# A two-layer encoder trunk: input in column pieces, later sums of the activations, attention's projection ahead of the convolution's

## The chip, the core and the metric

The kernel runs on one core of a Trainium2 chip. The metric is the device time of one execution in microseconds (us). Engines are called PE (TensorE), ACT (ScalarE), DVE (VectorE), POOL (GpSimd) and SP (SyncE, which issues most of the loads). Each takes its own instructions in order and waits for the others by semaphores.

## The reference

The input x has 512 rows of 1024 float32. Two layers, each with two feed-forward networks (FFN) around a mixer of attention and convolution:

```python
def reference(x, ...):
    for l in range(2):
        x = x + 0.5 * swiglu_ffn(rmsnorm(x, ffn1_norm[l]), ffn1_w_up[l], ffn1_w_down[l])
        x = x + mixer(rmsnorm(x, mix_norm[l]), w_in[l], ...)
        x = x + 0.5 * swiglu_ffn(rmsnorm(x, ffn2_norm[l]), ffn2_w_up[l], ffn2_w_down[l])
        x = rmsnorm(x, final_norm[l])

def swiglu_ffn(h, w_up, w_down):          # w_up 1024 x 5632, w_down 2816 x 1024
    a, b = split(h @ w_up); return (silu(a) * b) @ w_down

def mixer(h, ...):
    q, k, v, glu_in, gates = split(h @ w_in + b_in)
    outs, lses = dilated window attention of 3 groups of 8 heads (rms-normed, rotated q and k)
    wts = softmax over the 3 groups of lses
    y_attn = sum(wts * outs) (512 x 512) @ w_attn_proj (512 x 1024)
    y_conv = silu(layernorm(depthwise_conv31(glu))) @ w_conv_proj (1024 x 1024) + b_conv_proj
    g_attn, g_conv = split(sigmoid(gates))
    return (g_attn * y_attn + g_conv * y_conv) @ w_out
```

## The kernel before

**Layout.** The activations are held transposed, as eight tiles x0 to x7 of 128 features by 512 rows. Each activation that enters a product is split into a high and a low part (xgh and xgl, sh and sl for y, zh and zl for the convolution's result), made by ACT (a rounding copy, `hi`) and DVE (the difference, `lo`), and every weight tile too (`stage`: SP loads `raw`, ACT makes `hi`, DVE makes `lo`). A product is then three matmuls (`mm3`, L157 to L159). `proj_cols` runs such products for 256 columns of a weight at once, into two PSUM banks. The high and low parts of the weights have four buffers each, `raw` has two. A norm's scale is applied behind a product: R is the reciprocal root of the row's mean square, made by DVE and ACT and spread over the partitions by a matmul (`ps_bc`, L214).

**Start.** Four row tiles `xnat` (128 x 1024) are loaded by SP (L80), PE transposes them (`ps_x`, L721), ACT and DVE make xgh and xgl from the transposed banks (L174, L175), ACT squares the row tiles for the first norm (`sqn`, L727).

**FFN** (`ffn`). The up-projection is walked in pairs of column tiles m = 0, 2, 4 ... 20, in three PARTS of which each ends with its share of the down-projection. For m below 4 both halves a and b are plain products (banks `ps_a`, `ps_b`). From m = 4 on b is made by a seven-product scheme (`proj7`, banks `ps`), which needs sums of four quarter tiles of the activation: `sums7` (L269 to L271), from g = xgh + xgl (L324), split into Th and Tl; and likewise sums of the weights (`stage7`, `sm`, L251 to L253). After a pair DVE multiplies ps_a by R (L340), ACT applies silu, DVE multiplies by b (L345 or L343), and the result h is split. Layer 1's first FFN also runs `deferred`, the rescaling of x0 to x7 by the norm at the end of layer 0 (L780), behind the pair m = 0.

**Mixer** (`mixer`). Products with w_in and the attention of the three groups fill most of it; the convolution's 31 taps run on DVE meanwhile. Attention's unnormed results are written to device memory as `od`, twelve blocks of 128 x 512 (group by pair of heads), and come back at the end. That end, the combining of the heads, is: PE transposes the groups' weights (`ps_cT`, L665); ACT and DVE split them (`tmp`, L166 and L167); for each of four pairs of heads and three groups PE spreads the weights over the partitions (`ps_c`, two matmuls, L673 and L674), POOL loads a block of od into `oin` (L676, tag `ot` with four buffers), DVE multiplies (L677) and sums the three (L681); the sum is split into y (L166, L167). Then come the convolution's projection (`ps_cp`, 192 matmuls, needs z), whose product with the gate sgc stands at L689; attention's projection (`ps_ap`, 96 matmuls, needs y0 to y3), product with the gate sga (L698) and sum (L699), split into `mg`; and the output projection (`ps_o`).

**Order.** The code is written stage by stage; a scheduler places the instructions on the engines by priority (written order, with loads of weights and some norms pulled ahead), buffers of a pool and PSUM banks limit it. The placed order, not the written one, is what each engine runs.

## Time and profile before

| | us |
|---|---|
| median of three runs | 2653.77 (2652.79 to 2654.54) |
| the profiled execution | 2655.37 |
| its span in the trace | 2653.3 |
| PE busy in the span | 2593.0 |
| DVE busy | 1984.0 |
| ACT busy | 1100.8 |

The profile lists each instruction with its start, its duration, and, in brackets, how long its engine stood idle before it and which instruction or transfer ended that idle time. The ends of matmuls are modelled, so what one costs is read from the distance of two starts. PE waits have to be looked for one by one, since it is busy for 98% of the span.

### The profile page before, as it was taken

Reading aid. Unit: us, or ns where it says so; the run is one execution under the profiler, and the core shown is the slowest. Engines: PE = TensorE matmul, PEld = TensorE weight load, DVE = VectorE, ACT = ScalarE, POOL = GpSimd, SP = SyncE. Lnnn points to the kernel's source line nnn. Section 1 sums busy time; section 2 is a strip of 40 time slices with the busy share of each in tenths; the row PEclk is TensorE's granted clock in tenths of the full one; section 3 lists DMA queues with packets and bytes.
Section 4 is the critical chain, followed back from the end, with each engine's and each line's share of the span. In section 5 each row is a group of like instructions: output and inputs, shape, how many; then the busy total and the mean of one; then the engine's idle time right before and its main releaser. Section 6 shows DMA issues by size and latency. Waiting matters only on the chain.

```text
span 2653.3 us, 34486 instructions
## 1 busy us (share of the span) xinstructions
PE 2593.0 (98%) x13421; PEld 2168.9 (82%) x13421; DVE 1984.0 (75%) x3218; ACT 1100.8 (41%) x1651; POOL 110.8 (4%) x208
## 2 busy tenths in 40 slices
PE   8999999998999999999979999999999999999998
PEld 6888988776877788888868989887767777888887
DVE  6666669999986667666766766699999866666665
ACT  5333342243587234233433333422445773433334
POOL 1000000011011000000000000000011110000000
PEclk9999999999999999999989999999999999999999
DMA  4323333232333333232313333332323343233322
GB/s 143 104 92 108 92 108 105 84 119 89 108 108 113 111 96 104 88 111 91 101 55 111 96 104 96 103 105 88 110 88 120 104 129 104 88 104 96 108 92 80
DMA packets 245603, 268.87 MB, mean 101 GB/s; under 512 B 11624, under 2 KB 230128, under 8 KB 245440
## 3 DMA queue, kind: packets, MB, share of 16 engines
q1 hardware_dynamic: 233920, 234.91, 28.5%
q0 software_dynamic: 11504, 31.76, 4.1%
q8 instruction: 105, 1.72, 0.3%
q14 instruction: 58, 0.48, 0.1%
q10 hardware_dynamic: 16, 0.00, 0.0%
HBM read 251.75 MB, written 14.88 MB: 100 GB/s over the span
## 4 chain that ended last, share of the span: by engine, by line
PE 92%; DVE 6%; ACT 1%; issue 1%; DMA 0%; SPq 0%; ACTq 0%
PE ps_a L158 6%; PE ps_a L159 6%; PE ps_a L157 6%; PE ps_d L158 6%; PE ps_d L157 6%; PE ps_d L159 6%; PE ps L159 5%; PE ps L158 5%; PE ps L157 5%; PE ps_n L158 4%; PE ps_n L157 4%; PE ps_n L159 4%; DVE cv L620 2%; PE ps_S L528 1%; PE ps_pv L558 1%; PE ps_cp L158 1%
## 5 line engine op out<-in xcount | busy, mean ns | idle before, releaser
L152 ACT ACTIVATE hi<-raw 128x1024 fp32r<-128x1024 f32 (+1 forms) x376 | 391.5, 1042 | 698.1 <-PE ps_d L158 156.1
L153 DVE TENSOR_TENSOR lo<-raw,hi 128x1024 fp32r<-128x1024 f32 (+1 forms) x376 | 451.1, 1200 | 252.0 <-ACT hi L152 251.1
L620 DVE SCALAR_TENSOR_TENSOR cv<-u,cwc,cv 128x497 f32<-128x497 f32 (+14 forms) x480 | 335.8, 738 | 0.0
L157 PE MATMUL ps_a<-xgh,hi 128*128 128x512 f32 x704 | 275.7, 392 | 18.5 <-DVE t L340 16.2
L158 PE MATMUL ps_a<-xgl,hi 128*128 128x512 f32 x704 | 276.7, 393 | 0.6 <-DVE xgl L175 0.6
L159 PE MATMUL ps_a<-xgh,lo 128*128 128x512 f32 x704 | 276.2, 392 | 0.0
L158 PE MATMUL ps_d<-hl,hi 128*128 128x512 f32 x704 | 272.6, 389 | 0.0
L159 PE MATMUL ps_d<-hh,lo 128*128 128x512 f32 x704 | 272.6, 389 | 0.0
L157 PE MATMUL ps_d<-hh,hi 128*128 128x512 f32 x704 | 270.6, 389 | 0.0
L158 PE MATMUL ps_n<-lo,xgh 128*128 128x512 f32 x576 | 229.2, 398 | 4.2 <-DVE lo L153 4.2
L159 PE MATMUL ps_n<-hi,xgl 128*128 128x512 f32 x576 | 226.0, 393 | 0.0
L157 PE MATMUL ps_n<-hi,xgh 128*128 128x512 f32 x576 | 215.6, 396 | 4.6 <-DVE tmp L483 4.2
L157 PEld LDWEIGHTS ps_a<-xgh,hi 128*128 128x128 f32 x704 | 133.2, 189 | 46.2 <-DVE t L340 16.6
L158 PE MATMUL ps<-Tl,hi 128*128 128x256 f32 x576 | 163.0, 283 | 0.0
L159 PE MATMUL ps<-Th,lo 128*128 128x256 f32 x576 | 163.0, 283 | 0.0
L157 PE MATMUL ps<-Th,hi 128*128 128x256 f32 x576 | 162.8, 283 | 0.0
L159 PEld LDWEIGHTS ps_a<-xgh,lo 128*128 128x128 f32 x704 | 133.1, 189 | 28.4 <-issue 0.5
L158 PEld LDWEIGHTS ps_a<-xgl,hi 128*128 128x128 f32 x704 | 133.4, 190 | 27.6 <-DVE xgl L175 1.1
L157 PEld LDWEIGHTS ps_d<-hh,hi 128*128 128x128 f32 x704 | 132.2, 188 | 27.5
L159 PEld LDWEIGHTS ps_d<-hh,lo 128*128 128x128 f32 x704 | 132.1, 188 | 27.5
L158 PEld LDWEIGHTS ps_d<-hl,hi 128*128 128x128 f32 x704 | 132.1, 188 | 27.3
L166 ACT ACTIVATE hi<-sm 128x1024 fp32r<-128x1024 f32 x72 | 76.4, 1061 | 184.7 <-DVE sm L253 76.0
(266 smaller groups left out, 5506.5 us busy)
## 6 DMA issues: line engine op xcount, KB each, us to landing
raw<-in_ffn_w_up_dram SPq DMA_DIRECT2D x176, 512.0 KB, 3.5
raw<-in_w_in_dram SPq DMA_DIRECT2D x88, 512.0 KB, 3.7
raw<-in_ffn_w_down_dram SPq DMA_DIRECT2D x76, 512.0 KB, 3.4
raw<-in_w_in_dram SPq DMA_DIRECT2D x96, 256.0 KB, 3.2
raw<-in_w_conv_proj_dram SPq DMA_DIRECT2D x16, 512.0 KB, 3.4
raw<-in_w_out_dram SPq DMA_DIRECT2D x16, 512.0 KB, 3.4
vd<-tmp POOLq DMA_DIRECT2D x24, 256.0 KB, 2.4
od<-ot POOLq DMA_DIRECT2D x24, 256.0 KB, 3.2
```

The source lines that it names most:

```text
L152: nc.scalar.activation(hi[:, :m], raw[:, :m], AF.Copy)
L153: nc.vector.tensor_sub(lo[:, :m], raw[:, :m], hi[:, :m].bitcast(F32))
L157: nc.tensor.matmul(ps, ah, bh, start=first, stop=False)
L158: nc.tensor.matmul(ps, ah, bl, start=False, stop=False)
L159: nc.tensor.matmul(ps, al, bh, start=False, stop=last)
L166: nc.scalar.activation(hi, src, AF.Copy)
L528: nc.tensor.matmul(pS[e][:, w * n + lo:w * n + hi], qkT[hp, i, b * P:(b + 1) * P], qkT[hp, 2 + i, k0 + lo:k0 + hi], start=True, stop=True)
L558: nc.tensor.matmul(pv[e * 64:(e + 1) * 64, i, b - b2, :], V[b + j][:, (hh * UH + h) * HD:(hh * UH + h + 1) * HD], PT[e][:, (nj * w + j) * ...
L620: nc.vector.scalar_tensor_tensor(a[:, t0:t1], u[k][:, t0 + d:t1 + d], cw(l, j, k), a[:, t0:t1], op0=ALU.mult, op1=ALU.add)
```

## The change

Four edits. The input comes in four column pieces (all 512 rows, 256 columns each) of one tile instead of four row tiles. The sums of the activations for the seven-product scheme, in all four FFNs, are made behind the evacuation of the pair m = 0 instead of ahead of the first product, and the deferred rescale moves from behind m = 0 to behind m = 2. In the mixer, attention's projection is written ahead of the convolution's; its result is multiplied into the gate sga in place, and the convolution's evacuation then makes the merged sum. y0 to y3 and the low part of the merged result take other buffers (`sp`, `V`, `big`).

```diff
@@ -73,12 +73,12 @@
 
     x0s = ExitStack()
     x0 = x0s.enter_context(tc.tile_pool(name="x0", bufs=1))
-    xnat = []
-    for tt in range(TT):
-        t = x0.tile([P, D], F32, name=f"xnat{tt}")
-        with tc.high_priority():
-            nc.sync.dma_start(t, A["x"][0, tt * P:(tt + 1) * P, :])
-        xnat.append(t)
+    xn = x0.tile([P, TT, D], F32, name="xnat")
+    xsrc = A["x"][0].rearrange("(t p) d -> p t d", p=P)
+    with tc.high_priority():
+        for c in range(0, D, 256):
+            nc.sync.dma_start(xn[:, :, c:c + 256], xsrc[:, :, c:c + 256])
+    xnat = [xn[:, tt] for tt in range(TT)]
 
     grow = x0.tile([KD, P], F32, name="grow")
     nc.scalar.dma_start(grow, A["ffn1_norm"][0].rearrange("(k p) -> k p", p=P))
@@ -318,11 +318,6 @@
         with tc.tile_pool(name=uniq("ffn"), bufs=4) as fp:
             few.add(id(fp))
             x7 = []
-            for q in range(0, KD, 2):
-                t2 = fp.tile([P, 2, S], F32, tag="t2", name=uniq("g2"), bufs=2)
-                for j in range(2):
-                    nc.vector.tensor_add(t2[:, j], xg[q + j][0].bitcast(F32), xg[q + j][1].bitcast(F32))
-                x7.append(sums7(fp, t2, xg[q:q + 2], "T", 8))
             for m0, m1 in PARTS:
                 h = []
                 for m in range(m0, m1, 2):
@@ -346,7 +341,13 @@
                     h2 = split_to(*(fp.tile([P, 2, S], F32R, tag="h", name=uniq("h" + x), bufs=8) for x in "hl"), t2)
                     for j in range(2):
                         h.append(tuple(x[:, j] for x in h2))
-                    if m == 0 and deferred is not None:
+                    if m == 0:
+                        for q in range(0, KD, 2):
+                            t2 = fp.tile([P, 2, S], F32, tag="t2", name=uniq("g2"), bufs=2)
+                            for j in range(2):
+                                nc.vector.tensor_add(t2[:, j], xg[q + j][0].bitcast(F32), xg[q + j][1].bitcast(F32))
+                            x7.append(sums7(fp, t2, xg[q:q + 2], "T", 8))
+                    if m == 2 and deferred is not None:
                         deferred()
                 last = m1 == NF
 
@@ -679,29 +680,23 @@
                         acc = o
                     else:
                         nc.vector.tensor_add(acc, acc, o)
-                y.append(split(mp, acc, "big", NB))
-
+                y.append(split(mp, acc, *(("sp", 6) if pr < 3 else ("V", 5))))
+
+            for c in range(4):
+                ps = [ps_at(uniq("ps_ap")) for _ in range(2)]
+                proj_cols(wap, c * 256, y, 4, ps)
+                for j in range(2):
+                    nc.vector.tensor_mul(sga[2 * c + j], ps[j], sga[2 * c + j])
+            mg = []
             for c in range(4):
                 ps = [(ps_at if c % 2 else ps_mm)(uniq("ps_cp")) for _ in range(2)]
                 proj_cols(wcp, c * 256, z, KD, ps)
                 for j in range(2):
                     k = 2 * c + j
-                    nc.vector.scalar_tensor_tensor(sgc[k], ps[j], pc("b_conv_proj", l, k), sgc[k], op0=ALU.add, op1=ALU.mult)
-            mg = []
-            for c in range(4):
-                ps = [ps_at(uniq("ps_ap")) for _ in range(2)]
-                proj_cols(wap, c * 256, y, 4, ps)
-                ss = []
-                for j in range(2):
-                    k = 2 * c + j
                     s = slot("tmp", 7)
-                    nc.vector.tensor_mul(s, ps[j], sga[k])
-                    nc.vector.tensor_add(s, s, sgc[k])
-                    ss.append(s)
-                if c % 2 == 0:
-                    ml = mp.tile([P, 4, S], F32R, tag="qk", name=uniq("ml"), bufs=2)
-                for j in range(2):
-                    mg.append(split_to(slot("sgc", 8, F32R), ml[:, 2 * (c % 2) + j], ss[j]))
+                    nc.vector.scalar_tensor_tensor(s, ps[j], pc("b_conv_proj", l, k), sgc[k], op0=ALU.add, op1=ALU.mult)
+                    nc.vector.tensor_add(s, s, sga[k])
+                    mg.append(split_to(slot("sgc", 8, F32R), slot("big", NB, F32R, name="ml"), s))
             for ts in ((0, 1), (2, 3), (4, 5), (6,), (7,)):
                 ps = [(ps_at if ts[0] in (0, 4, 7) else ps_mm)(uniq("ps_o")) for _ in ts]
                 proj_cols(wou, ts[0] * P, mg, KD, ps)
```

PE's order in the mixer of layer 0, where the heads are combined. Before, from the last products of the gate (ps_gA) over the transposes (ps_cT) into the convolution's projection:

```order
L158 MATMUL ps_gA_6735<-xgl_3152,hi_6767 128x512
L159 MATMUL ps_gA_6735<-xgh_3151,lo_6768 128x512
L665 MATMUL ps_cT_7185<-ident,cg_7165 96x128 x4
L157 MATMUL ps_cp_7290<-zh_7117,hi_7293 128x512
L158 MATMUL ps_cp_7290<-zl_7118,hi_7293 128x512
L159 MATMUL ps_cp_7290<-zh_7117,lo_7294 128x512
L157 MATMUL ps_cp_7290<-zh_7123,hi_7293 128x512
L158 MATMUL ps_cp_7290<-zl_7124,hi_7293 128x512
```

After, the same place:

```order
L159 MATMUL ps_gA_6732<-xgh_3148,lo_6765 128x512
L666 MATMUL ps_cT_7182<-ident,cg_7162 96x128 x4
L674 MATMUL ps_c_7191<-tmp_7187,sel 128x512
L674 MATMUL ps_c_7197<-tmp_7187,sel 128x512
L674 MATMUL ps_c_7204<-tmp_7187,sel 128x512
L674 MATMUL ps_c_7215<-tmp_7187,sel 128x512
L675 MATMUL ps_c_7191<-tmp_7188,sel 128x512
L675 MATMUL ps_c_7197<-tmp_7188,sel 128x512
L675 MATMUL ps_c_7204<-tmp_7188,sel 128x512
L675 MATMUL ps_c_7215<-tmp_7188,sel 128x512
```

The convolution's matmuls that followed the transposes are gone from here: the spreading of the weights now comes directly behind, all 24 in a row. Before, the first ps_c came 28 matmuls later, and the others stood among ps_cp's.

PE's order a little further on, after; sh and sl are the parts of y0 (7211, 7212) and y1 (7235, 7236):

```order
L674 MATMUL ps_c_7276<-tmp_7187,sel 128x512
L675 MATMUL ps_c_7276<-tmp_7188,sel 128x512
L157 MATMUL ps_ap_7287<-sh_7211,hi_7290 128x512
L158 MATMUL ps_ap_7287<-sl_7212,hi_7290 128x512
L159 MATMUL ps_ap_7287<-sh_7211,lo_7291 128x512
L157 MATMUL ps_ap_7287<-sh_7235,hi_7290 128x512
L158 MATMUL ps_ap_7287<-sl_7236,hi_7290 128x512
```

Behind the last ps_c the attention projection begins; ps_cp, 192 matmuls, stands behind it except for one (in layer 1 four) of them.

DVE's order at the start of layer 1's first FFN, from the spread norm's diagonals (dg) on. Before:

```order
L212 TENSOR_SCALAR dg_11015<-ident,rsr_10990 128x128 x4
L153 TENSOR_TENSOR lo_11309<-raw_11307,hi_11308 128x1024
L324 TENSOR_TENSOR g_1821_11026<-xgh_10734,xgl_10735 128x512
L324 TENSOR_TENSOR g_1821_11026<-xgh_10745,xgl_10746 128x512
L324 TENSOR_TENSOR g_1825_11037<-xgh_10808,xgl_10809 128x512
L324 TENSOR_TENSOR g_1825_11037<-xgh_10821,xgl_10822 128x512
L251 TENSOR_TENSOR sm_11353<-raw_11352 128x512
L780 SCALAR_TENSOR_TENSOR x_81<-x_81,pcol,ps_bc_11020 128x512
```

After:

```order
L212 TENSOR_SCALAR dg_11018<-ident,rsr_10993 128x128 x4
L153 TENSOR_TENSOR lo_11304<-raw_11302,hi_11303 128x1024
L251 TENSOR_TENSOR sm_11356<-raw_11355 128x512
L335 TENSOR_TENSOR t_1843_11153<-ps_a_11029,R_11016 128x512
L335 TENSOR_TENSOR t_1843_11153<-ps_a_11030,R_11016 128x512
L348 TENSOR_TENSOR g_1846_11164<-xgh_10737,xgl_10738 128x512
L348 TENSOR_TENSOR g_1846_11164<-xgh_10748,xgl_10749 128x512
L251 TENSOR_TENSOR sm_11412<-raw_11411 128x512
```

Two of the sums g of four stand now behind the evacuation of ps_a (L335, before L340), which before had its place 38 rows behind the first g (L324); the rescales (L780, now L775) follow in both.

ACT's order at the start of the kernel. Before:

```order
L152 ACTIVATE hi_304<-raw_303 128x1024
L727 ACTIVATE sqn_221,ss_220<-xnat_92 128x1024
L727 ACTIVATE sqn_223,ss_220<-xnat_94 128x1024
L727 ACTIVATE sqn_225,ss_220<-xnat_96 128x1024
L727 ACTIVATE sqn_227,ss_220<-xnat_98 128x1024
L152 ACTIVATE hi_334<-raw_333 128x1024
L174 ACTIVATE xgh_145<-ps_x_140,gcol 128x512
```

After:

```order
L152 ACTIVATE hi_257<-raw_256 128x1024
L152 ACTIVATE hi_287<-raw_286 128x1024
L174 ACTIVATE xgh_142<-ps_x_137,gcol 128x512
L174 ACTIVATE xgh_152<-ps_x_147,gcol 128x512
L718 ACTIVATE x_81<-ps_x_137 128x512
L174 ACTIVATE xgh_162<-ps_x_157,gcol 128x512
L718 ACTIVATE x_82<-ps_x_147 128x512
L174 ACTIVATE xgh_172<-ps_x_167,gcol 128x512
L722 ACTIVATE sqn_218,ss_217<-xnat 128x1024
```

The four squares of the row tiles stood ahead of the first xgh; now four xgh stand ahead of the first square, and a second weight tile is split ahead of them.

## Rows read from the trace of the kernel before

**Rows 1.** The page: busy us (share) xinstructions, then the last chain by engine.

```profile
PE 2593.0 (98%) x13421; PEld 2168.9 (82%) x13421; DVE 1984.0 (75%) x3218; ACT 1100.8 (41%) x1651; POOL 110.8 (4%) x208
...
PE 92%; DVE 6%; ACT 1%; issue 1%; DMA 0%; SPq 0%; ACTq 0%
```

**Rows 2.** Table by window: length, busy us (count) of PE, PEld, DVE, ACT, POOL; clock.

```profile
848.00:866.00 18.00, 18.00 (x80) 12.55 (x79) 13.43 (x19) 7.44 (x11) 1.62 (x3) 1.00 0.43 132
866.00:869.00 3.00, 3.00 (x9) 2.35 (x8) 1.60 (x4) 0.63 (x1) 1.08 (x2) 0.50 0.87 250
...
1368.00:1384.00 16.00, 4.91 (x12) 3.84 (x13) 15.85 (x28) 7.94 (x10) 0.00 (x0) 0.50 0.11 33
1384.00:1386.00 2.00, 2.00 (x9) 1.61 (x8) 1.48 (x2) 1.98 (x2) 0.00 (x0) 0.82 0.00 0
```

**Rows 3.** Timeline of ACT, then PE, at the start: start, duration, instruction.

```profile
4.48 1.06 ACT L152 ACTIVATE hi<-raw 128x1024 fp32r<-128x1024 f32 x1 [1.80 <-DMA raw<-in_ffn_w_up_dram]
...
9.27 1.06 ACT L727 ACTIVATE sqn<-xnat 128x1024 f32<-128x1024 f32 x1 [3.73 <-DMA xnat<-in_x_dram]
...
14.39 1.82 ACT L174 ACTIVATE xgh<-ps_x,gcol 128x512 fp32r<-128x512 f32 x3
...
9.29 3.54 PE L721 MATMUL ps_x<-ident,xnat 128*128 128x128 f32 x16 [5.64 <-DMA xnat<-in_x_dram]
15.12 0.73 PE L157 MATMUL ps_a<-xgh,hi 128*128 128x512 f32 x2 [2.28 <-ACT xgh L174]
```

**Rows 4.** DMA issues of the first 22 us: KB each, median us to landing.

```profile
raw<-in_ffn_w_up_dram SPq DMA_DIRECT2D x5, 512.0 KB, 5.6
xnat<-in_x_dram SPq DMA_DIRECT2D x4, 512.0 KB, 6.6
```

**Rows 5.** Timeline of PE, then DVE, at layer 1's first FFN.

```profile
1362.48 0.39 PE L159 MATMUL ps_b<-xgh,lo 128*128 128x512 f32 x1
1379.09 0.79 PE L157 MATMUL ps_a<-xgh,hi 128*128 128x512 f32 x1 [16.22 <-DVE t L340]
1379.68 0.63 PE L158 MATMUL ps_a<-xgl,hi 128*128 128x512 f32 x1
1380.11 0.63 PE L159 MATMUL ps_a<-xgh,lo 128*128 128x512 f32 x1
...
1356.09 2.50 DVE L324 TENSOR_TENSOR g<-xgh,xgl 128x512 f32<-128x512 f32 x4 [9.19 <-PE ps_bc L214]
...
1378.36 1.88 DVE L340 TENSOR_TENSOR t<-ps_a,R 128x512 f32<-128x512 f32 x3
...
1391.83 1.22 DVE L167 TENSOR_TENSOR hl<-t,hh 128x1024 fp32r<-128x1024 f32 x1
```

**Rows 6.** Timeline of PE, then DVE, combining the heads in layer 0.

```profile
848.38 0.60 PE L665 MATMUL ps_cT<-ident,cg 128*96 128x128 f32 x4
...
870.21 0.39 PE L159 MATMUL ps_cp<-zh,lo 128*128 128x512 f32 x1
870.43 0.39 PE L157 MATMUL ps_cp<-zh,hi 128*128 128x512 f32 x1
...
853.31 0.68 DVE L167 TENSOR_TENSOR tmp<-ps_cT,tmp 96x512 fp32r<-96x512 f32 x1
...
857.82 2.48 DVE L677 TENSOR_TENSOR oin<-oin,ps_c 128x512 f32<-128x512 f32 x4 [1.19 <-PE ps_c L674]
...
864.00 0.68 DVE L167 TENSOR_TENSOR sl<-oin,sh 128x512 fp32r<-128x512 f32 x1
...
884.40 0.69 DVE L167 TENSOR_TENSOR sl<-oin,sh 128x512 fp32r<-128x512 f32 x1 [0.70 <-ACT sh L166]
```

**Rows 7.** Loads of od: POOL's issue, DVE's product, landing times of all 24.

```profile
864.98 0.54 POOL L676 DMA_DIRECT2D oin<-od  x1 [1.86 <-DVE sl L167]
...
868.92 0.69 DVE L677 TENSOR_TENSOR oin<-oin,ps_c 128x512 f32<-128x512 f32 x1 [1.36 <-DMA oin<-od]
...
DMA to landing us min/median/max: 2.8/3.1/5.4
```

## The prediction

> **What bounds the kernel now.** I read the page's busy times first: TensorE (PE) works 2593.0 of 2653.3 us, VectorE (DVE) 1984.0, ScalarE (ACT) 1100.8, and the chain of work that ended last is 92% PE [rows 1]. So PE is the bound, and the change adds and removes no matmul: 13,421 stay. It can gain only where PE idles or runs at the lower clock, some 60 us in all, and can lose wherever it makes PE wait. Then I went stage by stage with the table of windows. PE is fully busy through the combining of the heads (18.00 of 18.00 us) [rows 2], so the mixer's edit has nothing to win there. Two holes touch the change: the start, and the beginning of layer 1's first FFN, where PE stood still for 16.22 us for a DVE evacuation [rows 5] and the clock was at half (granted 0.50) [rows 2].
>
> The steady price of one 128x512 matmul is the distance of two starts: 870.43 - 870.21 = 0.22 us (0.227 over a longer stretch) at full clock [rows 6], and 1380.11 - 1379.68 = 0.43 us at half [rows 5]. After that hole PE ran from 1379.09 and the granted clock was a mean 0.82 over 1384 to 1386: the rise came some 5.2 us after the restart [rows 2, 5].
>
> **The change, part 1: the input in column pieces.** Before, all of ps_x waits until 9.29 us for the row tiles of x, ACT then squares all four of them (first at 9.27), and only at 14.39 makes the first xgh, so the first projection matmul starts at 15.12 [rows 3]. With column pieces the first two transposable columns land before the rest, and in the new order ACT makes xgh ahead of the squares. A second weight load now goes ahead of x on SyncE's queue. The first weight tile's split began at 4.48 when it had landed, the four row tiles were there by 9.29 [rows 3], so a place of 512 KB in this queue costs about 1.2 us; I put the first piece at some 7 us, the second at 8.2, sixteen transposes end near 10 (0.22 us each, 3.54/16 [rows 3]), and the first matmul of ps_a comes 5 us sooner. The remaining transposes now stand between the matmuls, and ACT has the same 4 us of squares to do a little later, with PE's 24 first matmuls (some 8 us, partly at half clock) to cover them. I take 5 us gained; the ends are 0 (the pieces land together, the squares then hold xgh of the later columns back) and 8.
>
> A weight tile moves as 1 KB runs and x before as 4 KB runs, and both are 512 KB: 5.6 against 6.6 us from issue to landing [rows 4]. The short runs show no price here. The Trainium skill, "DMA: Bandwidth & Descriptors", section "Why small descriptors are slow (HBM only)", says against the change that each packet carries a fixed overhead of about three cycles beside one per 32 bytes. By it (an estimate) 35 cycles per KB against 131 per 4 KB make x 7% slower, some 0.3 us of the gain; the rows decide, and I take none.
>
> **Part 2: the sums of later activations behind the first evacuation.** Thirty-two adds and sixteen groups of differences in four FFNs change place; none is removed. At three of the starts PE had no idle time, so there is nothing to gain. At layer 1's first FFN the DVE begins its queue at 1356.09, when the broadcast of R arrives, and is then busy without a real break until hl at 1391.83 + 1.22 = 1393; in that queue the first evacuation of ps_a stands at 1378.36, behind 22 us of sums and rescales [rows 5]. The new order puts the two evacuations at some 1356.7, so PE goes on at 1362.7 instead of 1379.09. But the same some 35 us of DVE work must still be done, from the same start, and PE's next matmuls need its results: summed by the order with the durations of the trace (0.60 per 128x512 step, 1.14 per 128x1024), the last Tl is ready at about 1391, the bank evacuations of the next pair at 1383. After PE's 24 free matmuls and 4 more (6 us, until 1368.5) it advances in pieces. By about 1391 it can have done some 85 of the next 132 matmuls, and the rest (21 of 0.12 us, 26 of 0.227, with some waits for banks) end at 1400 to 1406, against 1408.4 before. I take 4 us gained, ends 0 and 9. The deferred rescale (eight steps, 5.3 us) stands in the same queue in both.
>
> **Part 3: the attention projection in front.** Before, behind the transposes of the head weights (848.38 to 848.98) PE has the convolution's projection to run while the chain of the heads goes its slow way: split of the weights (DVE until 853.99), the spread matmuls ps_c, products (857.82), sums, split of y0 (until 864.68), and so on to y3 at 884.40 + 0.69 = 885.09 [rows 6]. These 36 us cost PE nothing. In the new order the 24 ps_c follow the transposes at once, then the attention projection, which needs y0 to y3; the convolution's 192 matmuls, the cover, stand behind it. An engine takes its instructions in order, so PE waits.
>
> How long: ps_c can start at 854.0. Products of the first pair follow at about 854.9 (0.6 us each), sums end at 858.7, y0 is split by 860. Each further y needs loads of od into buffers that the y before releases: after sl ended at 864.68, GpSimd issued at 864.98 and the product followed at 868.92 [rows 6, 7], so 0.3 + 3.9 us, and with the median landing of 3.1 us [rows 7] some 3.4. A product and a sum more (1.3 us) make a step of 4.7 to 5.5 us; I take 5.3. Three steps from 858.7, and 1.3 us for the split: y3 at about 876. In before, y0 to y3 took 20.4 us with other work on DVE; that is the upper bound, y3 at 880.4. Thirty-one of the projection's 96 matmuls stand ahead of the first that needs y3, but their banks come free with the ninth product or later, so between 65 and 80 are left at 876. Either 12 of 65 at half clock (5.2 us) and 53 at 0.227, or 78 at 0.227: the projection ends at about 893.5. Without a wait the same work would end at 848.98 + 24 x 0.17 + 96 x 0.227 = 874.8. PE loses 18.7 us, less the 1.4 us that before already lost at half clock (866 to 869, granted 0.50 [rows 2], seven matmuls at 0.2 more): **17 us per layer**. Every microsecond of y3 is one of the loss: 14 with y3 at 873, 22 with 880.4. Layer 1 has the same chain with the same durations (the 24 loads of both layers stand in one row [rows 7]), so 34 us, from 28 to 44.
>
> The Trainium skill, "SBUF — State Buffer", section "The DMA setup-cost knee", gives a transfer some 2 us and its bytes by 436 GB/s: 2.6 us for these 256 KB (an estimate). By it a step would be 4.2 us, y3 at 873, and the sum 6 us lower. The rows show 2.8 at least and 3.1 in the median [rows 7]; they decide.
>
> The rest of the part is free: the convolution's projection, once begun, has z from before; its weights wait for staging buffers that the attention projection frees one by one, 5.4 us apart, ACT and DVE need 2.3 us per tile, and both have time there. The product into the gate in place removes no instruction. Attention's own stretch shifts by a few instructions: 0, ends -3 and 3.
>
> **Sum.** +34 - 4 - 5 = +25 us on 2655.37; the median of the runs is 1.6 us lower, so 2653.77 + 25 = 2679. Ends by the bounds: +28 - 9 - 8 - 3 = +8 and +44 + 3 = +47.
>
> **Rivals.** (a) *The hole in layer 1's FFN closes entirely*: PE never waits again once the bank is free, and gets back 16.22 us and the 12 half-clock matmuls (2.5 us): +34 - 19 - 5 = +10, 2664. For it: the hole's releaser is just the evacuation that moves. Against: the DVE's queue behind it. It decides if the last Tl is ready by 1372 rather than 1391.
> (b) *The faster side: y is ready before PE gets to it*, because the chain's loads run ahead of the sums that release their buffers and no hole opens: -4 - 5 = -9, 2645. It turns faster once the loss per layer is under 4.5 us, y3 by 863.5, that is three steps in 4 us. One load lands in 2.8 us at the least [rows 7] and the third step's waits for the second's sums, which speaks against it; only four buffers are there.
> (c) *The change does not do what it says*: the scheduler keeps convolution matmuls between the ps_c and the loss vanishes while the start gains nothing either: +0, 2654. The order of the new kernel shows no such matmul, so this has little left.
> (d) *The bubble costs more*, since the convolution's weights come late behind it or the attention stretch meets a new wait: 5 us per layer more, +35, 2689; inside the range.
>
> **How the numbers follow.** Forecast with (d) 0.76, (a) 0.10, (b) 0.08, (c) 0.06. About 0.2% (5.3 us) is what a measurement here can tell from no change. Faster: (b) and a little of (a) with the low ends, 0.10. Same: (c) and low ends, 0.07. Slower: 0.83. The range holds the forecast's bounds and (a) and leaves out (b), (c) and the last of the upper end: 2661 to 2697.
>
> **What would show it.** In the profile of the changed kernel: PE idle between about 849 and 876 us in layer 0 and again in layer 1 (shifted), released by DVE sl or the product, with a granted clock near 0.5 there, and some 60 matmuls of ps_ap after it; in layer 1's first FFN no 16 us wait on the evacuation but several smaller waits on Tl, lo and banks to about 1390; the first ps_a matmul near 10 us. The forecast is wrong if PE is over 90% busy in those two mixer stretches, or if y3 comes by 865.

## The result, and the profile after

The changed kernel takes 2686.07 us (median of four runs, 2684.43 to 2687.16) against 2654.02 us for the kernel before (median of four, the three of the table above and one more): **slower**, ratio 1.0121 (95% interval 1.0108 to 1.0133). The forecast of 2679 us with a range of 2661 to 2697 and 0.83 for slower holds. Its parts hold less well than its sum: one is 8 us too large, another 12 us too small.

The profiled execution took 2685.75 us (span 2683.4). Its busy times, which answer to [rows 1]:

```profile
PE 2606.8 (97%) x13421; PEld 2177.9 (81%) x13421; DVE 1987.1 (74%) x3218; ACT 1108.1 (41%) x1656; POOL 110.8 (4%) x208
```

PE has the same 13,421 matmuls, 13.8 us more busy time (the granted clock is at half for 95.7 us of the span, against 56.8) and, since the span grew by 30.1 us, 16.3 us more idle time. The table follows the same matmul in both traces: the first start of a stage's bank, after minus before, and what the stage in front of it added.

| first matmul of | before | after | difference | added by the stage |
|---|---|---|---|---|
| layer 0's mixer (ps_gg) | 373.2 | 370.1 | -3.1 | -3.1 start and first FFN |
| transposes of the head weights, layer 0 (ps_cT) | 848.4 | 849.1 | +0.8 | +3.9 attention, layer 0 |
| output projection, layer 0 (ps_o) | 923.6 | 936.7 | +13.2 | **+12.4** combining and projections |
| down-projection of layer 1's first FFN (ps_d) | 1429.3 | 1439.0 | +9.7 | -3.4 that FFN's beginning |
| ps_cT, layer 1 | 2167.9 | 2185.6 | +17.7 | **+8.0** attention, layer 1 |
| ps_o, layer 1 | 2241.5 | 2272.4 | +31.0 | **+13.2** combining and projections |
| end of the span | 2653.3 | 2683.4 | +30.1 | -0.8 |

The list of what PE waited for (engine line waited for: us in total, times, longest) names the same places. Before, its first row was the 16.22 us of [rows 5]; that row is gone:

```profile
PE ps_T L551 <- ACT sp L548: 11.7, 9, 2.9
PE ps_c L674 <- DVE oin L678: 9.0, 6, 3.5
...
PE ps_c L674 <- ACT tmp L166: 6.5, 2, 3.3
```

The waits of ps_c are the combining of the heads; ps_T, transposes in attention, had 5.9 us before.

**Combining the heads, layer 0.** PE's timeline (start, duration, instruction, idle before it and what ended it), which answers to [rows 6]:

```profile
849.14 0.60 PE L666 MATMUL ps_cT<-ident,cg 128*96 128x128 f32 x4
853.00 0.73 PE L674 MATMUL ps_c<-tmp,sel 8*128 8x512 f32 x4 [3.26 <-ACT tmp L166]
...
868.82 0.77 PE L157 MATMUL ps_ap<-sh,hi 128*128 128x512 f32 x1 [0.37 <-DVE oin L678]
...
893.22 0.39 PE L159 MATMUL ps_ap<-sh,lo 128*128 128x512 f32 x1
```

and the DVE's, with the products and the four splits of y:

```profile
855.63 2.48 DVE L678 TENSOR_TENSOR oin<-oin,ps_c 128x512 f32<-128x512 f32 x4 [0.89 <-PE ps_c L675]
...
860.13 0.69 DVE L167 TENSOR_TENSOR sl<-oin,sh 128x512 fp32r<-128x512 f32 x1 [0.69 <-ACT sh L166]
861.84 0.69 DVE L678 TENSOR_TENSOR oin<-oin,ps_c 128x512 f32<-128x512 f32 x1 [1.01 <-DMA oin<-od]
...
865.27 0.69 DVE L167 TENSOR_TENSOR sl<-oin,sh 128x512 fp32r<-128x512 f32 x1
...
870.09 0.69 DVE L167 TENSOR_TENSOR sl<-oin,sh 128x512 fp32r<-128x512 f32 x1
...
874.86 0.69 DVE L167 TENSOR_TENSOR sl<-oin,sh 128x512 fp32r<-128x512 f32 x1 [0.70 <-ACT sh L166]
```

PE transposes at 849.14, waits 3.26 us for the weights' split, then for products; y3 is split at 874.86 + 0.69 = 875.55, and the last matmul of the attention projection starts at 893.22. Before, PE ran the convolution's projection all that time. The table by window (length, busy us and count of PE, PEld, DVE, ACT, POOL, then the granted clock, the DMA share and GB/s) shows the price in clock:

```profile
849.00:854.00 5.00, 1.47 (x10) 0.68 (x8) 3.48 (x5) 4.55 (x8) 0.00 (x0) 0.98 0.03 11
854.00:869.00 15.00, 9.28 (x21) 4.70 (x22) 11.53 (x19) 1.26 (x2) 3.76 (x7) 0.50 0.46 140
869.00:874.00 5.00, 5.00 (x12) 3.96 (x13) 4.33 (x7) 0.63 (x1) 0.54 (x1) 0.50 0.38 105
874.00:878.00 4.00, 4.00 (x18) 3.28 (x17) 0.85 (x2) 0.63 (x1) 0.00 (x0) 0.97 0.00 0
```

In the 15 us from 854 PE is busy for 9.28, at half clock, and the clock stays there until 874, some 5 us after PE got steady work at 868.82.

**Layer 1's first FFN.** PE, and then the DVE, answering to [rows 5]:

```profile
1384.53 0.38 PE L157 MATMUL ps<-xgh,hi 128*128 128x256 f32 x1 [1.62 <-ACT hi L166]
...
1389.03 0.58 PE L159 MATMUL ps<-xgh,lo 128*128 128x256 f32 x1 [2.03 <-DVE lo L167]
...
1394.60 0.80 PE L157 MATMUL ps<-Th,hi 128*128 128x256 f32 x2 [1.47 <-ACT Th L166]
1397.38 0.58 PE L158 MATMUL ps<-Tl,hi 128*128 128x256 f32 x1 [1.99 <-DVE Tl L167]
```

```profile
1369.26 0.69 DVE L251 TENSOR_TENSOR sm<-raw 128x512 f32<-128x512 f32 x1 [9.20 <-PE ps_bc L214]
1369.87 1.28 DVE L335 TENSOR_TENSOR t<-ps_a,R 128x512 f32<-128x512 f32 x2
...
1403.19 1.22 DVE L167 TENSOR_TENSOR Tl<-ts,Th 128x1024 fp32r<-128x1024 f32 x1
```

One wait of 16.2 us has become seven of 0.5 to 2 us; the four longest rows are shown. The evacuation of ps_a now comes at 1369.87 right behind the broadcast, but the DVE's queue still runs from 1369.26 to the last Tl at 1403.19 + 1.22 = 1404.4, and PE waits for the queue's results one by one.

### The profile page after: what moved, and what is told of

It is laid out like the page before. It is cut to its first block, busy times and chain, and to the rows that moved or that the text cites. A ratio compares the mean times of both kernels' runs of the same rounds, so it can differ in the third digit from the quotient of the medians.

```text
span 2683.4 us, 34476 instructions
## 1 busy us (share of the span) xinstructions
PE 2606.8 (97%) x13421; PEld 2177.9 (81%) x13421; DVE 1987.1 (74%) x3218; ACT 1108.1 (41%) x1656; POOL 110.8 (4%) x208
## 4 chain that ended last, share of the span: by engine, by line
PE 60%; DVE 6%; ACT 1%; issue 1%; DMA 0%; DVEq 0%; SPq 0%; ACTq 0%
PE ps_d L158 4%; PE ps_d L159 4%; PE ps_d L157 4%; PE ps_a L158 4%; PE ps_a L157 4%; PE ps_a L159 4%; PE ps L158 3%; PE ps L159 3%; PE ps L157 3%; DVE cv L621 2%; PE ps_n L158 1%; PE ps_n L157 1%; PE ps_n L159 1%; PE ps_o L159 1%; PE ps_cp L159 1%; PE ps_cp L158 1%
## 5 line engine op out<-in xcount | busy, mean ns | idle before, releaser
L166 ACT ACTIVATE hi<-raw 128x1024 fp32r<-128x1024 f32 x72 | 76.4, 1060 | 197.7 <-PE ps_d L158 69.4
```

The costliest lines, as they stand in the source:

```text
L166: nc.scalar.activation(hi, src, AF.Copy)
```

## The experiments

The stage differences below are read as in the table, against the first trace of before.

### The mixer's edit undone, and alone

Undone (the code of before from y to the merged sum, the rest as changed):

```diff
-                y.append(split(mp, acc, *(("sp", 6) if pr < 3 else ("V", 5))))
+                y.append(split(mp, acc, "big", NB))
...
+            (convolution's projection, then attention's, as before)
```

> The changed kernel with the mixer's edit undone (input pieces, later sums and later rescale stay). In the trace of the changed kernel the start gained 3.1 us, layer 1's first FFN 3.5, the tail 0.9; the two stretches from the head weights' transposes to the output projection lost 12.4 and 13.2; attention's stretch lost 3.8 (layer 0) and 8.0 (layer 1). Theory A (the loss in attention comes from where the scheduler puts attention's matmuls, which shifts with any edit): layer 0 has PE's order of the changed kernel there and keeps the 3.8, layer 1 has an order of its own, 0 to 8 lost: 2654 - 7.5 + 3.8 to 11.8 = 2650 to 2658. Rival B (the loss in attention comes from the mixer's edit, by its buffers): both vanish, 2646.5. In both the two stretches behind the transposes show no idle PE.

Measured: 2652.8 us, ratio 0.9994 (0.9985 to 1.0004). Stages: start -2.6, attention of layer 0 +2.3, combining and projections -1.6 and 0.0, layer 1's FFN -4.8, attention of layer 1 +0.7.

Alone (the code of before, with the changed lines from y to the merged sum):

> The kernel before with the mixer's edit alone. Theory A: the 25.6 us behind the transposes, attention of layer 0 in the order of before (0), layer 1 in an order of its own (0 to 8): 2680 to 2688. Rival B: 25.6 + 11.8 = 2691.

Measured: 2685.48 us, ratio 1.0123 (1.0108 to 1.0138). Stages: combining and projections +12.2 and +13.6, attention +0.1 and +7.6. So the whole loss comes with the mixer's edit, and 25.7 us of it are in the stretch behind the transposes. The other edits take 9.5 us off the start, layer 1's FFN, the projections and the tail of this trace and add 3.0 in attention; but the profiled execution was the fastest of its ten (2648.92), and by the medians the kernel differs from before by no more than the measurement can tell. Both times lie where theory A put them. With the mixer's edit alone layer 0's attention did not lengthen, which speaks against rival B; layer 1 needed a run of its own.

### The convolution in front, the new buffers kept

```diff
             for c in range(4):
-                ps = [ps_at(uniq("ps_ap")) for _ in range(2)]
-                proj_cols(wap, c * 256, y, 4, ps)
+                ps = [(ps_at if c % 2 else ps_mm)(uniq("ps_cp")) for _ in range(2)]
+                proj_cols(wcp, c * 256, z, KD, ps)
...
-                proj_cols(wcp, c * 256, z, KD, ps)
+                proj_cols(wap, c * 256, y, 4, ps)
```

> The changed kernel with the convolution's projection in front again, while y, the low part of the merged result and the merged sum keep the new buffers. If the place of the projection is the cause of the stretch behind the transposes (theory), the time is that of the kernel without the mixer's edit within 2 us. If the new buffers cost time (rival: y in buffers shared with attention, the low part in those of the convolution's inputs), it lies above it by up to the 25 us.

Measured: 2651.93 us, ratio 0.9996 (0.9986 to 1.0005), 0.9 us from the kernel without the mixer's edit. Combining and projections: -1.6 and 0.0. The buffers are free; the place of the projection costs.

### Part of the cover put back, and the loads of od ahead

The first quarter of the convolution's projection in front of attention's, three quarters behind:

```diff
+            for c in range(1):
+                (projection and product with sgc of column pair c, in place)
             for c in range(4):
                 ps = [ps_at(uniq("ps_ap")) for _ in range(2)]
...
-            for c in range(4):
+            for c in range(1, 4):
```

> The changed kernel with the first quarter of the convolution's projection (48 matmuls, 10.9 us at full clock) ahead of attention's, the other three quarters behind it. Theory (PE has nothing to run while y0 to y3 are made): the quarter fills 10.9 us of the hole and keeps the clock up for some of it, so of the 12.4 and 13.2 us lost behind the transposes 1 to 4 are left in each layer: 2662 to 2670, layer 1's attention in another order again (-8 to +3 on that). Rival (the new place of the projection costs by its banks or weight buffers, not by a missing cover): the two stretches keep 10 us or more.

Measured: 2670.3 us, ratio 1.0064 (1.0047 to 1.008). The stretches lost 5.5 and 7.3 instead of 12.4 and 13.2: 48 matmuls of cover buy 7 and 6 us of their 10.9. More than the 1 to 4 us expected is left, since the chain itself became longer: the first products came at 857.28 instead of 855.63, behind matmuls of the quarter, and between them and y0 the DVE evacuated two banks of it (859.67 and 861.66, 0.74 us each) and split a weight tile (862.32, 1.22). y3 was ready at 878.70 + 0.69, 4 us later than in the changed kernel, and PE still waited for products:

```profile
PE ps_c L674 <- DVE oin L678: 5.6, 3, 2.7
```

The rival (10 us or more stay) falls. Then the chain itself, shortened. More buffers of `ot` have no room: with six, the mixer's pool needs 109.5 KB per partition where 106.6 are left. So the fifth to twelfth block go into the eight buffers that the convolution's results leave:

```diff
-                    o = slot("ot", 4, name="oin")
+                    o = slot("ot", 4, name="oin") if 3 * pr + g < 4 else slot("big", NB, name="oin")
```

> The changed kernel, but the fifth to twelfth block of attention's results go into the eight buffers that the convolution's results leave, so that all twelve loads stand ahead of the products. In the changed kernel y0 to y3 of layer 0 ended at 860.8, 866.0, 870.8 and 875.5. Theory of the prediction (each y waits for loads into buffers that the y before releases): what is left is DVE's own work, 12 products, 8 sums and 4 splits of 0.6 us from 855.6, some 14.4 us, so y3 at about 871 and 4 to 5 us less per layer: 2686 - 9 = 2677, apart from the order of attention's matmuls in layer 1, which is another one again (-8 to +3). Rival (loads are hidden, the chain is DVE's, ACT's and the spreading matmuls'): y3 stays within 1 us, 2686 apart from that order.

Measured: 2663.54 us, ratio 1.0039 (1.0024 to 1.0054). POOL's timeline: the loads now follow the splits of z, from 845.18, and the last one is issued before any product:

```profile
845.18 0.54 POOL L677 DMA_DIRECT2D oin<-od  x1 [1.58 <-DVE zl L167]
...
854.03 0.54 POOL L677 DMA_DIRECT2D oin<-od  x1 [1.20 <-DMA oin<-od]
```

and the DVE's splits of y0 to y3:

```profile
863.01 0.69 DVE L167 TENSOR_TENSOR sl<-oin,sh 128x512 fp32r<-128x512 f32 x1
...
866.01 0.69 DVE L167 TENSOR_TENSOR sl<-oin,sh 128x512 fp32r<-128x512 f32 x1
...
868.54 1.47 DVE L167 TENSOR_TENSOR sl<-oin,sh 128x512 fp32r<-128x512 f32 x2
```

The last row holds two, y2 and y3, so y3 is ready at 868.54 + 1.47 = 870.0 instead of 875.55, and the stretches lost 6.2 and 6.6 instead of 12.4 and 13.2. The loads that waited for buffers of the y before were thus half of the hole. The other half is the DVE's own 24 steps, which now follow each other with hardly a pause (busy 14.09 of the 15 us from 854); PE still waits 3.9 us for the weights' split and 0.9 us for products, and its clock is granted at a mean of 0.59 in these 15 us. The time fell by more than the 13 us of the two stretches because layer 1's attention came out in yet another order (0.0 instead of +8.0).

### Whose are the 8 us in attention?

The kernel before with the input's edit alone was run since its placed order of PE in layer 1's attention (the sequence of banks from the first ps_qT to ps_cT) is that of the changed kernel, with no edit of the mixer at all:

> The kernel before with the input in column pieces alone, no edit of FFN or mixer. Its placed order of attention in layer 1 is that of the changed kernel. Theory A (attention's loss of 8.0 us in layer 1 belongs to that order, whichever edit brings it about): the stretch from the first w_in product to the head weights' transposes is 6 to 9 us longer there than in before; the start gains 3; layer 0's attention has an order of its own, 0 to 4 longer: 2653 - 3 + 6 to 13 = 2656 to 2663. Rival B (it belongs to the mixer's buffers): layer 1's attention within 3 us of before and the time 2650 to 2654.

Measured: 2657.87 us, ratio 1.0013 (1.0004 to 1.0023). Layer 1's attention: +8.0 us, the same as in the changed kernel; start -4.8; layer 0's attention -1.8. What PE waited for in that stretch, before, changed, and here:

```profile
PE ps_T L550 <- ACT sp L547: 2.6, 3, 1.7
```

```profile
PE ps_T L551 <- ACT sp L548: 7.5, 5, 2.9
```

```profile
PE ps_T L550 <- ACT sp L547: 7.6, 6, 2.9
```

Theory A holds. PE waits for ACT's `sp` 5 us longer, and the other 3 us are busy time (371.15 us busy before, 374.36 changed, 374.71 here). That part stays open: the clock was at half for 13.7 us of this stretch both before and in the changed kernel. What the order does is seen at the longest of the waits, at the same transposes of the probabilities (those behind a row of 14 ps_pv), before and changed:

```profile
1966.33 3.38 DVE L620 SCALAR_TENSOR_TENSOR cv<-u,cwc,cv 128x510 f32<-128x510 f32 x5
...
1970.74 0.93 PE L550 MATMUL ps_T<-ident,sp 128*128 128x128 f32 x4 [0.28 <-ACT sp L547]
```

```profile
1976.17 6.00 DVE L621 SCALAR_TENSOR_TENSOR cv<-u,cwc,cv 128x508 f32<-128x508 f32 x9
...
1982.55 0.51 ACT L548 ACTIVATE sp<-sp,st 128x256 f32<-128x256 f32 x1 [3.38 <-DVE st L542]
...
1983.20 1.18 PE L551 MATMUL ps_T<-ident,sp 128*128 128x128 f32 x4 [2.90 <-ACT sp L548]
```

Nine of the convolution's taps (`cv`) instead of five stand on the DVE ahead of the masking of the scores (L541, now L542), whose `st` ACT's `sp` needs. The run with the input's edit alone has the same nine taps and the same wait (2.89). ACT also loads its tables more often in that order: from ps_gg to ps_cT of layer 1 it runs 25 ACT_TABLE_LOAD instructions of 1.28 us each, against 21. Over the orders below the price goes roughly with that number (19 loads: 0.0; 21: -3.0 to 3.3; 23: 2.9 to 7.5; 25: 7.6 to 8.0), but no run changed the loads alone, so they are not shown to be the cause. All runs, grouped by that placed order, in us added to attention:

| layer 0: kernels of one order | added |
|---|---|
| before, its second trace, mixer alone, early pool on before | 0.0, 0.1, 0.1, -0.2 |
| changed, no mixer's edit, convolution first, rescale late, early loads, one pair in front, early pool on changed | 3.9, 2.3, 2.2, 2.3, 3.1, 2.7, 4.0 |
| pieces alone, pieces and early pool | -1.8, -1.9 |
| later sums alone | 0.3 |

| layer 1: kernels of one order | added |
|---|---|
| before, its second trace, early pool on before | 0.0, -3.0, -1.4 |
| changed, pieces alone | 8.0, 8.0 |
| mixer alone | 7.6 |
| no mixer's edit, convolution first, rescale late | 0.7, 3.3, 3.1 |
| one pair in front, early pool on changed, later sums alone | 5.3, 5.7, 7.5 |
| early loads | 0.0 |
| pieces and early pool | 2.9 |

An order keeps its price within some 3 us; kernels with quite different edits that share it share the price. Why the scheduler comes to another order in layer 1 after an edit in the first microseconds was not traced.

How far one execution can be trusted was measured by a second trace of the unchanged kernel:

> The kernel before, unchanged, for a second trace of it. What differs between its two traces in each stage is what single executions differ by: under 1 us in the stages with a busy PE, and up to 3 in attention's, if the spread of 2649.7 to 2655.7 of its runs sits there (theory); evenly spread over all stages otherwise.

Measured: 2652.47 us. Every stage was within 0.1 us of the first trace but layer 1's attention, at -3.0. The theory holds, by this one pair: stage differences of 1 us outside attention count, and in layer 1's attention 3 may be chance. The granted clock differs there: it was at half for 13.7 us of that stretch in the first trace and for 6.8 in the second.

### The hole in layer 1's first FFN

First, the deferred rescale later:

```diff
-                    if m == 2 and deferred is not None:
+                    if m == 6 and deferred is not None:
```

(on the kernel without the mixer's edit)

> The kernel without the mixer's edit, with the deferred rescale of layer 1's first FFN (eight DVE steps, 5.3 us) behind the pair m = 6 instead of m = 2. Theory (what PE waits for there is the length of DVE's queue from the broadcast on): the queue ends 5.3 us earlier, the first down-projection of that FFN starts 4 to 7 us sooner than without this edit, and the time is 2652.8 - 5 = 2648, faster than the kernel before by some 5. Rival (ACT's or the weights' steps are late next): under 2 us.

Measured: 2652.0 us, ratio 0.9995 (0.9986 to 1.0004); that FFN -4.4, as without the edit (-4.8). The run does not decide: in the DVE's timeline the rescales (x) stand where they stood, right behind the first rows after the broadcast, so the edit did not change the placed order that it was to change:

```profile
1354.72 0.69 DVE L251 TENSOR_TENSOR sm<-raw 128x512 f32<-128x512 f32 x1 [9.20 <-PE ps_bc L214]
...
1358.34 3.38 DVE L781 SCALAR_TENSOR_TENSOR x<-x,pcol,ps_bc 128x512 f32<-128x512 f32 x5
```

The first row shows the other end of the queue: the DVE is idle for 9.20 us until the broadcast's matmul has read `dg`, whose buffer lies where the next FFN's pool begins. The same wait stands in [rows 5] (9.19). Taking dg out of that pool starts the queue earlier:

```diff
-        dg = pool.tile([P, S], F32, tag="tmp", name=uniq("dg"), bufs=tmps(pool))
+        dg = rp.tile([P, S], F32, tag="R", ...) if pool is None else pool.tile([P, S], F32, tag="tmp", ...)
...
-                    st["R"] = broadcast_cols(rt, "R", pool)
-                    R1 = broadcast_psum(r1, pool)
+                    R1 = broadcast_psum(r1, None)
+                    st["R"] = broadcast_cols(rt, "R", None)
```

On the kernel before:

> The kernel before, where the diagonal for the broadcast of the norms at the end of layer 0 takes the buffer of R instead of one in the FFN's pool, so that the next FFN's buffers need not wait for that broadcast; the rescale's broadcast goes first. In before the DVE stood idle for 9.2 us ahead of its queue of sums and rescales, and PE then waited 16.2 us for the evacuation behind them. Theory (the hole in layer 1's first FFN is the DVE's queue, from its start on): the queue starts some 9 us earlier, the evacuation comes at about 1369 instead of 1378, the hole shrinks by 7 to 10 us and some of the half clock with it; attention keeps its order in both layers: 2653 - 8 to 11 = 2642 to 2645. Rival (what follows, ACT's split and the weights, would be late anyway): under 3 us.

Measured: **2639.81 us, ratio 0.9945 (0.9928 to 0.9961)**. DVE, and then PE:

```profile
1342.32 2.49 DVE L324 TENSOR_TENSOR g<-xgh,xgl 128x512 f32<-128x512 f32 x4
...
1348.81 4.69 DVE L780 SCALAR_TENSOR_TENSOR x<-x,pcol,ps_bc 128x512 f32<-128x512 f32 x7
...
1366.64 1.88 DVE L340 TENSOR_TENSOR t<-ps_a,R 128x512 f32<-128x512 f32 x3
```

```profile
1367.38 0.79 PE L157 MATMUL ps_a<-xgh,hi 128*128 128x512 f32 x1 [5.11 <-DVE t L340]
```

The sums begin at 1342.32 instead of 1356.09, the rescales at 1348.81, the evacuation comes at 1366.64 instead of 1378.36, and PE waits 5.11 us instead of 16.22. The edit also puts the rescale's broadcast first. The sums read neither broadcast, so their earlier start is the buffer's; how much the order of the broadcasts gives the rescales was not separated. The FFN's beginning takes 12.4 us less, somewhat more than the 7 to 10 expected for the hole. The theory holds.

On the changed kernel without the mixer's edit:

> The same edit on the changed kernel without its mixer's part: the sums stand behind the first evacuation, the rescales now fill the idle time ahead of the broadcast of R. The waits of PE that were left there (9.7 us in seven pieces, the last till 1382) and their half clock end 6 to 9 us earlier by the theory: 2652 - 6 to 9 = 2643 to 2646, moved by up to 5 where layer 1's attention has another order once more. Rival as above: under 3 us.

Measured: 2653.32 us, ratio 0.9994 (0.9985 to 1.0004). The FFN's beginning gained 8.2 us against 4.8 without the edit, so 3.4 and not 6 to 9. PE still waits for sums:

```profile
1373.57 0.39 PE L158 MATMUL ps<-Tl,hi 128*128 128x256 f32 x1 [2.58 <-DVE Tl L167]
...
1376.87 0.80 PE L157 MATMUL ps<-Th,hi 128*128 128x256 f32 x2 [2.52 <-ACT Th L166]
1379.65 0.58 PE L158 MATMUL ps<-Tl,hi 128*128 128x256 f32 x1 [1.99 <-DVE Tl L167]
```

Here the sums stand behind the first evacuation by the code, so only the rescales moved into the idle time, while in before's code the sums themselves do. The later sums, which helped while the queue began with the broadcast, hinder once it begins earlier. Attention in an order at +5.7 took the rest.

Two parts together, the input's pieces and the early pool on the kernel before:

> The kernel before with the input in column pieces and the early pool, no later sums and no mixer's edit. From the stages measured one by one: start -4.8, layer 0's attention in the order of the run with the pieces alone -1.8, layer 1's first FFN -12.4, tail -0.5: 19.5 us less in the trace, if layer 1's attention, in an order not run before, costs nothing: 2654 - 19 = 2635. Theory (stages add, orders decide attention): 2632 to 2643, the latter with an order that costs 8. Rival (the gains share one cover): 2639 or more with attention unchanged.

Measured: 2638.99 us (2636.74 to 2644.44), ratio 0.9947 (0.993 to 0.9963). Start -4.4, layer 0's attention -1.9, the FFN -12.2: these stages add as the theory says; layer 1's attention came at +2.9, against -1.4 with the early pool alone, and so the two kernels measure alike. Both beat before and after.

### The start

The kernel before with the later sums alone:

> The kernel before with the later sums and the later rescale alone. If the sums behind the first evacuation delay the first FFN's seven-product scheme (theory), the start up to the first product with w_in loses the 1.7 to 2 us by which the changed kernel's start (-3.1) lags that with the pieces alone (-4.8); otherwise 0. Layer 1's first FFN gains 3.4 to 4.8. Attention has an order of its own in layer 0.

Measured: 2656.69 us. The start: -1.1, not a loss, so that theory falls; the FFN -4.6; attention of layer 1 +7.5. What separates -4.8 (pieces alone) from -3.1 (changed) is seen in PE's first rows. Changed:

```profile
8.37 3.68 PE L716 MATMUL ps_x<-ident,xnat 128*128 128x128 f32 x16 [4.72 <-DMA xnat<-in_x_dram]
11.69 1.20 PE L157 MATMUL ps_a<-xgh,hi 128*128 128x512 f32 x2
```

Pieces alone:

```profile
6.09 1.97 PE L721 MATMUL ps_x<-ident,xnat 128*128 128x128 f32 x8 [2.43 <-DMA xnat<-in_x_dram]
...
9.75 0.70 PE L157 MATMUL ps_a<-xgh,hi 128*128 128x512 f32 x2
```

With the pieces alone only the first weight tile stands ahead of x on SP's queue, and the transposes start at 6.09; the later sums bring the second weight tile's load ahead of x too, and they start at 8.37.

## Why the prediction was right or wrong, point by point

**The sum**: +25 forecast, +32 measured (+30.1 in the trace). Right in sign and range, but partly by luck: two of its terms are wrong with opposite signs.

**Part 3, combining the heads: right in mechanism, over-priced.** Forecast 17 us per layer (14 to 22), measured 12.4 and 13.2, below the lower end. y3 was put at 876 and came at 875.55; the projection's end was put at 893.5 and its last matmul started at 893.22. Of the two ways to price the projection's rest the second came true (78 matmuls at 0.227): PE had steady work from 868.82, and the clock was full again at 874.2, ahead of y3. (The clock's rise behind the hole of the kernel before came 5.6 us after the restart and not 5.2: the mean of 0.82 over 1384 to 1386 puts it at 1384.7.) The term that failed is the reference without a wait, 874.8: it counted 24 spreading matmuls at 0.17 us each, a price of rows of four in a row. Among other matmuls they cost 0.33: without the dip in clock the stretch from ps_cT to ps_o took 73.6 us (the kernel without the mixer's edit), of which 288 matmuls at 0.227 are 65.4, and the rest, 8, is theirs. In the changed kernel they lie in the hole and cost nothing. That is 4 us per layer. A smaller error is the 1.4 us taken off for half clock in both layers: layer 1 of the kernel before had no such dip (73.6 us, against 75.2 in layer 0). The mechanism is shown twice, by cover put back and by loads put ahead; the loads' steps were priced at 5.3 us and measured 5.1, 4.8 and 4.8 (865.27, 870.09 and 874.86 after 860.13).

**Attention: wrong.** "0, ends -3 and 3" stood against 3.9 + 8.0. The failing step is "shifts by a few instructions: 0": the order was seen to differ and was given no price, though PE waits there for chains over DVE and ACT, in which a few instructions more ahead of one step cost 2.6 us at a single place (2.90 against 0.28). The seven orders of layer 1 that were run lay between -3.0 and +8.0. This and part 3's error have opposite signs, so that the sum is better than its terms is luck.

**Part 2, later sums: right.** 4 us forecast (0 to 9), 3.4 measured (4.6 as the only edit), and by the reason given: the DVE's queue, not the place of the evacuation in it. The evacuation was put at 1356.7 and the last Tl at about 1391; less the 13.2 us by which the queue begins later in the changed kernel (1369.26 against 1356.09) they came at 1356.7 and 1391.2. Rival (a), the hole closes entirely, did not happen. What the prediction misread is why the queue begins when it does: it took 1356.09 for the arrival of the broadcast of R, but the sums at its head do not read R; they waited for the buffer of `dg`. That was worth 12 us.

**Part 1, the input: right in mechanism, size off.** 5 forecast, 3.1 measured, 4.8 for the pieces alone. The first transposes came at 8.37, not 7, and the first ps_a matmul at 11.69, not 10, since the second weight tile ahead of x held them for 2.3 us (8.37 against 6.09), more than the place of 1.2 us that was counted.

**The pages.** On short runs: with one weight tile ahead in both, x came 6.9 us (median) after issue as 1 KB pieces (the kernel with the pieces alone) and 6.6 as 4 KB rows. The difference of 0.3 us is the size that was estimated from the Trainium skill's "DMA: Bandwidth & Descriptors", section "Why small descriptors are slow (HBM only)". It does not show that cause: the same pieces at the same place of the queue took 7.4 us in the kernel with the pieces and the early pool. The lower price of a load that was estimated from the Trainium skill's "SBUF — State Buffer", section "The DMA setup-cost knee" (2.6 us, a step of 4.2 us), is not what y's steps of 4.8 to 5.1 show.

**Rivals.** (b) and (c) did not come true: PE was idle where forecast, 5.72 of the 15 us from 854. (d) asked for a new wait in attention or behind the hole; attention's was the part of it that came.

## What to carry to other kernels

Work that PE does beside a slow chain of small steps is cover, and moving it behind the chain costs the chain's length less what was slack. Price the hole from the moment PE runs dry to the moment the last input is ready, and the reference from a run without the hole. A queue on another engine is shortened from its start before its order is touched: ask what ended the idle time ahead of its first step, which here was a buffer of the pool before. Where a scheduler places the work, any edit can change the order of a far stage, so read that stage's own time in both traces, look at what stands ahead of the steps that the bounding engine waits for, and give it a price in the range.

## What the runs showed of the hardware

The granted clock can fall while PE is never idle. In before, at full PE time, it was below 1 behind a run of spreading matmuls (their weights have 8 rows, 8*128 in the timeline), and in the kernel without the mixer's edit, with the same matmuls a little differently spaced, it was not. Before (windows as above):

```profile
862.00:866.00 4.00, 4.00 (x16) 1.98 (x15) 3.83 (x6) 1.07 (x2) 1.47 (x3) 0.99 0.59 157
864.00:868.00 4.00, 4.00 (x14) 2.52 (x13) 3.35 (x6) 0.35 (x1) 1.23 (x3) 0.74 0.85 268
866.00:870.00 4.00, 4.00 (x13) 3.13 (x12) 2.60 (x5) 0.63 (x1) 1.08 (x2) 0.58 0.89 279
```

Without the mixer's edit:

```profile
862.00:866.00 4.00, 4.00 (x16) 1.97 (x15) 3.45 (x6) 0.85 (x2) 1.25 (x3) 1.00 0.55 172
864.00:868.00 4.00, 4.00 (x19) 2.72 (x16) 3.10 (x5) 0.22 (x1) 1.10 (x3) 1.00 0.71 248
866.00:870.00 4.00, 4.00 (x20) 3.27 (x18) 2.53 (x5) 1.32 (x2) 1.07 (x2) 1.00 0.77 265
```

That dip is 1.6 us of the stretch (75.2 against 73.6 us from ps_cT to ps_o) and belongs to no edit's purpose: in every trace without a hole, in either layer, the stretch takes the one or the other. The other surprise is how steady the rest is: outside layer 1's attention the two traces of the kernel before agree to 0.1 us at every stage over 2650 us.
